# An MLP up projection computed with seven block products instead of eight, with the residual stream kept in DRAM

## The chip, the cores and the metric

The kernel runs on one core of a Trainium2 chip. The metric is the device time of one execution in microseconds (us), lower is better. Its engines are named as the profile names them: PE (TensorE matmuls), PEld (TensorE weight loads), DVE (VectorE), ACT (ScalarE), POOL (GpSimd) and SP (SyncE, which issues nearly all transfers). Each engine works through its own instructions in the order of the program and waits for others by semaphores; a compiler-side scheduler fixes that order when the kernel is built.

## What is computed

One layer of a hybrid backbone for 512 latent tokens (and 256 context tokens) with 2048 channels: two groups of recurrent heads, an output projection, then an MLP with a depthwise convolution on an 8 x 64 grid. All data is 32-bit float. The change is in the MLP:

```python
def conv_ffn(h, rows, cols, w_up, conv_w, conv_b, w_down):
    u = jnp.einsum('btd,df->btf', h, w_up)                 # 2048 -> 2 x 5504
    u_gate, u_val = jnp.split(u, 2, axis=-1)
    g = lax.conv_general_dilated(u_gate.reshape(b, rows, cols, D_FF), conv_w[:, :, None, :], ...)
    g = g.reshape(b, t, D_FF) + conv_b
    return jnp.einsum('btf,fd->btd', jax.nn.silu(g) * u_val, w_down)
...
    x = x + gt1 * merge_groups(lat_gla, lat_ml, lat_gates[0], lat_gates[1], ...)
    h2 = rmsnorm(x, g_norm2) * (1 + sc2) + sh2
    x = x + gt2 * conv_ffn(h2, rows, GRID_W, w_up, conv_w, conv_b, w_down)
    return rmsnorm(x, g_final)
```

`sc2`, `sh2`, `gt1` and `gt2` come from a modulation, a product of one vector with a 2048 x 12288 matrix.

## The kernel before

Channels or features lie on the 128 partitions, tokens along the free dimension. The 2048 channels are 16 tiles of 128 (`KT`), the 5504 MLP features 43 tiles (`NF`), the tokens 512 columns (`T`).

Precision. PE multiplies in a reduced float format. `split` (L88) makes two parts of a tensor: ACT casts it to the high part (line L89 of the profile), DVE subtracts that from the original for the low part (L90). `mm3` (L104) then runs three matmuls for one product: high weight with high data, high weight with low data, low weight with high data. The third is the first that reads the low part of the weight. `mm` (L95) is the line of nearly all matmuls in the profile.

Weights. `load_split` (L160) is the only way in for weights: a transfer of 512 KB on SP into one of four `wraw` buffers, then a split into one of two `whi` and one of two `wlo` buffers. A split can therefore run one load ahead of PE. `unit` (L186) multiplies 16 channel tiles by up to four output tiles and takes eight such loads. After each load it runs a few `fillers`: pieces of the modulation (`mod_chunk`, L242), each with a transfer into `wraw`, a sum on DVE, a scaling on ACT and a sum of 512 columns on POOL (L257). `rate` says how many run per load. Of the modulation's parts, 2, 3 and 4 are made ahead of the MLP and part 5 (`gt2`) during its first units.

Stages. After the heads come the gate projections (`ga` in the profile), the output projection (`wo`) and the residual stream `x2`, 16 tiles in SBUF. Its norm gives `h2`, held as 16 high and 16 low tiles. The MLP then runs over eleven groups of up to four feature tiles (`QUADS`). `up_gate` (L1028) makes the gate features of a group (`ug`): ACT copies each from PSUM into a padded grid `pad`, ACT makes the first of nine convolution taps, DVE the other eight (L1043), ACT the SiLU. `up_val` (L1048) makes the value features (`uv`); DVE multiplies (L83) and the result is split into `gh` and `gl`, the input of the down projection. After two groups of up work `down_block` (L1064) runs for four blocks of 512 output channels (`dn`) and adds the result, times `gt2`, to `x2` (`residual`, L952). The last three groups go down together, and the last block of them (`dl`) is cut in two token ranges, so that the final norm can begin early.

All loads, splits, taps and matmuls are ordered by the scheduler; parts under `tc.high_priority()` come first where they are ready. PSUM has six accumulators of 512 columns for this.

Of the kernel before, what the change touches and what calls it, by code (L numbers as in the profile page):

```python
# [11 lines left out]
F32 = mybir.dt.float32  # L12
F32R = mybir.dt.float32r
# [5 lines left out]
P = 128  # L19
# [17 lines left out]
QUADS = [4] * 10 + [3]  # L37
GROUPS = [[0, 1], [2, 3], [4, 5], [6, 7], [8, 9, 10]]
# [31 lines left out]
def block_kernel(ctx: ExitStack, tc: tile.TileContext, a: dict, out: bass.AP):  # L70
# [48 lines left out]
    actp = pool(ctx, "actp")  # L119
    yp = pool(ctx, "yp")  # L120
    psA = pool(ctx, "psA", 6, PSUM)
# [16 lines left out]
    def ytile(k, name, shape=(P, T)):  # L138
        return yp.tile(list(shape), F32, name=name, tag=f"y{k}")
# [18 lines left out]
    rate, credit = [0], [0]  # L158

# [82 lines left out]
    def mod_chunk(region, n, kp, parts):  # L242

        name = f"m{region}_{n}_{kp}"
        raw = wraw.tile([P, 2, T], F32, name=f"raw_{name}", tag="raw")
        nc.sync.dma_start(raw, a["w_mod2"][region - 2, n, kp])
        if kp == 0:
            parts += [sum_tile(i, name) for i in range(2)]
        dv, po = parts
        ce, co = (csil[:, 2 * kp + i : 2 * kp + i + 1] for i in range(2))  # L250
        if kp == 0:
            V.tensor_scalar(out=dv, in0=raw[:, 0, :], scalar1=ce, scalar2=None, op0=ALU.mult)
            S.activation(po, raw[:, 1, :], AF.Copy, scale=co)
        else:
            V.scalar_tensor_tensor(out=dv, in0=raw[:, 0, :], scalar=ce, in1=dv, op0=ALU.mult, op1=ALU.add)  # L255
            S.activation(raw[:, 1, :], raw[:, 1, :], AF.Copy, scale=co)  # L256
            G.tensor_tensor(out=po, in0=po, in1=raw[:, 1, :], op=ALU.add)  # L257
        if kp == KP - 1:
            G.tensor_tensor(out=po, in0=po, in1=dv, op=ALU.add)
# [616 lines left out]
    mod_fillers((2, 3, 4), 3)  # L876
# [34 lines left out]
    for h in range(1, 2 * H):  # L911
        if h + 1 < 2 * H:
            accs = [acc(f"a{h + 1}_{g}", BANKS[g]) for g in range(6)]
            steps = project_steps(h + 1, accs)
        else:
            rate[0] = 1.5
            accs = [acc(f"ga0_{i}") for i in range(4)]
            steps = unit_steps(a["w_gates"][0], "ga0", *hx, accs)
        weave(first_stages(tiles) if h == 1 else stages(h, tiles), steps)
        for _ in steps:  # L920
            pass
        if h + 1 < 2 * H:
            tiles = evict(h + 1, accs)
# [8 lines left out]
    rate[0] = 1.5  # L932
# [19 lines left out]
    def residual(k, ps, gate, sl=slice(0, T)):  # L952
        xx = x2[k][:, sl]
        V.scalar_tensor_tensor(out=xx, in0=ps, scalar=gate[:, k : k + 1], in1=xx, op0=ALU.mult, op1=ALU.add)
# [27 lines left out]

    sums2 = []
    for n in range(4):
        accs = unit(a["w_out"][n], f"wo{n}", yh, yl)
        with tc.high_priority():
            for i in range(4):
                residual(4 * n + i, accs[i], modc[2])
                square(4 * n + i, sums2, rp, "sq")
# [3 lines left out]
    h2 = ([], [])  # L993
    with tc.high_priority():
        for k in range(KT):
            t = gp.tile([P, T], F32, name=f"h2_{k}", tag="h2")
            sk, bk = modc[4][:, k : k + 1], modc[3][:, k : k + 1]
            h2[0].append(acttile(k, "h", f"h2h{k}"))
            h2[1].append(acttile(k, "l", f"h2l{k}"))
            mul(t, x2[k], r2)  # L1000
            S.activation(h2[0][k], t, AF.Identity, scale=sk, bias=bk)  # L1001
            V.tensor_scalar(out=t, in0=t, scalar1=sk, scalar2=bk, op0=ALU.mult, op1=ALU.add)
            sub(h2[1][k], t, h2[0][k].bitcast(F32))
    st_3.close()
    st_h.close()


    fp = pool(ctx, "fp")
    tp = pool(ctx, "tp", 4)
# [4 lines left out]
    pads = [fp.tile([P, ROWS + 2, GW + 2], F32, name=f"pad{i}") for i in range(4)]  # L1014
    for p in pads:
        G.memset(p, 0.0)
    gs = {}
    LAST = 4 * GROUPS[-1][0]
    glast = fp.tile([P, NF - LAST, P], F32, name="glast")

    def sum_tile(i, name):
        return fp.tile([P, T], F32, name=f"sum{i}_{name}", tag=f"g{'hl'[i]}10")

    rate[0] = 1.5
    fillers += [lambda: None] * 20
    mod_fillers((5,), 2)

    def up_gate(q):  # L1028
        accs = unit(a["w_up4"][2 * q] if q < 10 else a["w_up3"][0], f"ug{q}", *h2, n=QUADS[q])
        convs = []  # L1030
        for i, ps in enumerate(accs):
            f = 4 * q + i
            with tc.high_priority():
                S.copy(pads[i][:, 1 : ROWS + 1, 1 : GW + 1], ps.rearrange("p (r c) -> p r c", c=GW))
            t = tp.tile([P, T], F32, name=f"cv{f}", tag="cv")
            t3 = t.rearrange("p (r c) -> p r c", c=GW)
            for tap in range(9):
                src = pads[i][:, tap // 3 : tap // 3 + ROWS, tap % 3 : tap % 3 + GW]
                w = cwt[:, f, tap : tap + 1]
                if tap == 0:  # L1040
                    S.activation(t3, src, AF.Identity, scale=w, bias=cbt[:, f : f + 1])  # L1041
                else:
                    V.scalar_tensor_tensor(out=t3, in0=src, scalar=w, in1=t3, op0=ALU.mult, op1=ALU.add)  # L1043
            S.activation(t, t, AF.Silu)
            convs.append(t)
        return convs

    def up_val(q, convs):  # L1048
        accs = unit(a["w_up4"][2 * q + 1] if q < 10 else a["w_up3"][1], f"uv{q}", *h2, n=QUADS[q])
        for i, ps in enumerate(accs):  # L1050
            f = 4 * q + i
            with tc.high_priority():
                mul(convs[i], convs[i], ps)
                gh = fp.tile([P, T], F32R, name=f"gh{f}", tag=f"gh{f % 8 if q < 10 else 8 + i}")
                gl = fp.tile([P, T], F32R, name=f"gl{f}", tag=f"gl{f % 8 if q < 10 else 8 + i}")
                split(gh, gl, convs[i])
            gs[f] = (gh, gl)
            if f >= LAST:
                S.copy(glast[:, f - LAST, :], convs[i][:, 3 * P :])

    def fspan(qs):
        return [f for q in qs for f in range(4 * q, 4 * q + QUADS[q])]

    def down_block(fs, blk):  # L1064
        accs = [acc(f"dn{fs[0]}_{blk}_{i}") for i in range(4)]
        for p in range(0, len(fs), 2):
            pair = fs[p : p + 2]
            wh, wl = load_split(a["w_down"][blk][:, pair[0] : pair[0] + len(pair), :], f"d{pair[0]}_{blk}", n=len(pair))
            for i in range(4):
                for ff, f in enumerate(pair):  # L1070
                    mm3(accs[i], wh[:, ff, P * i : P * i + P], wl[:, ff, P * i : P * i + P],
                        gs[f][0], gs[f][1], f == fs[0], f == fs[-1])
        with tc.high_priority():
# [15 lines left out]
    fs = fspan(todo[0])  # L1089
    parts = [slice(0, 3 * P), slice(3 * P, T)]  # L1090
    sums3 = [[], []]
    for blk in range(3):
        down_block(fs, blk)
        for k in range(4 * blk, 4 * blk + 4):
            for pt, sl in enumerate(parts):
                square(k, sums3[pt], fp, f"fq{pt}", sl)
            S.activation(x2[k], x2[k], AF.Copy, scale=gnf[:, k : k + 1])

    wd = []
    for n, f in enumerate(fs):  # L1100
        if n < 10:
            raw = actp.tile([P, T], F32, name=f"raw_dl{f}", tag=f"a{'hl'[n % 2]}{11 + n // 2}")
        else:
            raw = fp.tile([P, T], F32, name=f"raw_dl{f}", tag="wlast")
        wh, wl = acttile(n, "h", f"dlh{f}"), acttile(n, "l", f"dll{f}")
# [5 lines left out]
    for pt, sl in enumerate(parts):  # L1111
# [10 lines left out]
        with tc.high_priority():  # L1122
            for i in range(4):
                residual(12 + i, accs[i], modc[5], sl)
                square(12 + i, sums3[pt], fp, f"fq{pt}", sl)
            r3 = token_rstd(sums3[pt], fp, f"rmsf{pt}", w)
            r3s = fp.tile([P, w], F32, name=f"r3s{pt}", tag=f"r3s{pt}")
# [17 lines left out]
def arrange(x, c, ctx, c_ctx, w_mod, b_mod, g_norm1, g_norm2, w_in, gla_w_lr, gla_b_lr, mlstm_b_gate,  # L1145
# [44 lines left out]
    for d in range(2):  # L1190
# [3 lines left out]
    r["w_up4"] = np.stack([blocks(w_up[:, FF * s + 512 * q : FF * s + 512 * q + 512], 512)  # L1194
                           for q in range(10) for s in range(2)])
    r["w_up3"] = np.stack([blocks(w_up[:, FF * s + 5120 : FF * s + 5504], 384) for s in range(2)])
# [20 lines left out]
```

## Time and profile before

| | us |
|---|---|
| median of 3 runs | 2595.97 (2594.4 to 2598.1) |
| profiled execution | 2598.67 |
| its span | 2597.0 |
| mean granted PE clock | 0.993 of full |

The time is that of the whole execution; the span runs from its first to its last recorded instruction, so 1.7 us lie around it. The page gives the busy time of each engine and the chain of work that ended last. Matmuls are pipelined: the mean length of one matmul record (some 390 ns for 512 columns) is longer than the distance between two of them, and it is the distance that counts. The lines themselves are shown where the prediction uses them.

### The profile page before, as it was taken

How to read it: one execution, taken by the hardware profiler on the slowest of the kernel's cores; microseconds unless marked ns; L12 is line 12 of the kernel's file. 1: busy time of each engine (PE TensorE's matmuls, PEld its weight loads, DVE VectorE, ACT ScalarE, POOL GpSimd, SP SyncE). 2: the span in 40 equal slices, each digit the busy share in tenths (PEclk: the TensorE clock that was granted, in tenths of full speed). 3: DMA queues.
4: the chain of work that ended last, by engine and by line, in shares of the span. 5: the costliest groups of instructions: out<-in, count | busy, mean ns of one | idle time of the engine just before them, and what ended most of it. 6: DMA issues, size and time to landing. Idle time of an engine off the chain costs nothing.

```text
span 2597.0 us, 31782 instructions
## 1 busy us (share of the span) xinstructions
PE 2530.0 (97%) x12782; PEld 2132.0 (82%) x12782; DVE 1361.3 (52%) x1972; ACT 873.7 (34%) x1289; POOL 225.8 (9%) x179
## 2 busy tenths in 40 slices
PE   6998999999999999999999999999999999999998
PEld 4887898888897887878878888888888888888887
DVE  6566765543344465458576326533653365336643
ACT  4224543333334344334443123312331233123431
POOL 0000000111212323210321000000000000000000
PEclk9999999999999999989999999999999999999999
DMA  8751012231333566633554333333233323333431
GB/s 322 282 204 41 30 44 81 69 96 64 130 119 126 205 233 221 192 121 100 208 186 138 97 98 98 98 97 97 98 97 96 96 95 97 97 97 90 141 90 65
DMA packets 96676, 321.96 MB, mean 124 GB/s; under 512 B 11152, under 2 KB 15504, under 8 KB 96528
## 3 DMA queue, kind: packets, MB, share of 16 engines
q1 hardware_dynamic: 95376, 319.40, 37.5%
q8 instruction: 100, 1.64, 0.3%
q10 hardware_dynamic: 1152, 0.52, 0.1%
q14 instruction: 48, 0.39, 0.0%
HBM read 315.69 MB, written 4.19 MB: 123 GB/s over the span
## 4 chain that ended last, share of the span: by engine, by line
PE 89%; DVE 5%; DMA 3%; issue 1%; ACT 1%; SPq 0%; POOL 0%; DVEq 0%; ACTq 0%; POOLq 0%
PE ug L95 18%; PE uv L95 17%; PE dn L95 17%; PE a L95 16%; PE wo L95 6%; PE ga L95 5%; PE po L95 3%; DMA raw_m<-in_w_mod 2%; PE sl L95 1%; PE dl L95 1%; PE ps_m L95 1%; DVE cv L1043 1%; DMA raw_h<-in_w_heads 1%; PE s L95 0%; PE cst L95 0%
## 5 line engine op out<-in xcount | busy, mean ns | idle before, releaser
L95 PE MATMUL ug<-h2h,hi_ug 128*128 128x512 f32 x688 | 269.0, 392 | 1.6 <-ACT h2h L1001 1.6
L95 PE MATMUL uv<-h2h,lo_uv 128*128 128x512 f32 x688 | 268.8, 391 | 1.6 <-DVE lo_uv L90 1.6
L95 PE MATMUL uv<-h2h,hi_uv 128*128 128x512 f32 x688 | 268.6, 390 | 1.2 <-ACT hi_uv L89 1.2
L95 PE MATMUL ug<-h2l,hi_ug 128*128 128x512 f32 x688 | 268.3, 390 | 0.0
L95 PE MATMUL uv<-h2l,hi_uv 128*128 128x512 f32 x688 | 268.2, 390 | 0.0
L95 PE MATMUL ug<-h2h,lo_ug 128*128 128x512 f32 x688 | 268.2, 390 | 0.0
L95 PE MATMUL dn<-gh,hi_d 128*128 128x512 f32 x644 | 250.5, 389 | 0.0
L95 PE MATMUL dn<-gl,hi_d 128*128 128x512 f32 x644 | 250.5, 389 | 0.0
L95 PE MATMUL dn<-gh,lo_d 128*128 128x512 f32 x644 | 250.5, 389 | 0.0
L1043 DVE SCALAR_TENSOR_TENSOR cv<-pad,cwt,cv 128x512 f32<-128x512 f32 x344 | 242.5, 762 | 10.6 <-ACT cv L1041 9.1
L90 DVE TENSOR_TENSOR lo_ug<-raw_ug,hi_ug 128x1024 fp32r<-128x1024 f32 (+1 forms) x88 | 106.5, 1210 | 240.1 <-ACT hi_ug L89 240.1
L257 POOL TENSOR_TENSOR sum_m<-sum_m,raw_m 128x512 f32<-128x512 f32 x112 | 175.3, 1566 | 578.2 <-ACT raw_m L256 358.4
L90 DVE TENSOR_TENSOR lo_uv<-raw_uv,hi_uv 128x1024 fp32r<-128x1024 f32 (+1 forms) x88 | 105.9, 1203 | 177.5 <-ACT hi_uv L89 177.1
L90 DVE TENSOR_TENSOR lo_d<-raw_d,hi_d 128x1024 fp32r<-128x1024 f32 x82 | 98.8, 1205 | 166.5 <-ACT hi_d L89 165.5
L89 ACT CAST hi_ug<-raw_ug 128x1024 fp32r<-128x1024 f32 (+1 forms) x88 | 90.9, 1033 | 266.6 <-PE ug L95 196.4
L89 ACT CAST hi_d<-raw_d 128x1024 fp32r<-128x1024 f32 x82 | 85.0, 1037 | 280.4 <-PE dn L95 231.8
L255 DVE SCALAR_TENSOR_TENSOR sum_m<-raw_m,csil,sum_m 128x512 f32<-128x512 f32 x112 | 97.6, 871 | 156.1 <-DMA raw_m<-in_w_mod 155.9
L89 ACT CAST hi_uv<-raw_uv 128x1024 fp32r<-128x1024 f32 (+1 forms) x88 | 90.9, 1033 | 246.4 <-PE uv L95 181.3
L95 PEld LDWEIGHTS uv<-h2h,lo_uv 128*128 128x128 f32 x688 | 129.4, 188 | 30.2 <-DVE lo_uv L90 3.2
L95 PEld LDWEIGHTS ug<-h2h,hi_ug 128*128 128x128 f32 x688 | 129.8, 189 | 28.8 <-ACT h2h L1001 1.9
L95 PEld LDWEIGHTS uv<-h2h,hi_uv 128*128 128x128 f32 x688 | 129.5, 188 | 28.3 <-ACT hi_uv L89 1.6
L95 PEld LDWEIGHTS ug<-h2h,lo_ug 128*128 128x128 f32 x688 | 129.6, 188 | 27.2
(308 smaller groups left out, 5178.7 us busy)
## 6 DMA issues: line engine op xcount, KB each, us to landing
raw_m<-in_w_mod SPq DMA_DIRECT2D x192, 512.0 KB, 4.4
raw_ug<-in_w_up SPq DMA_DIRECT2D x80, 512.0 KB, 3.4
raw_uv<-in_w_up SPq DMA_DIRECT2D x80, 512.0 KB, 3.4
raw_d<-in_w_down SPq DMA_DIRECT2D x79, 512.0 KB, 3.5
raw_h<-in_w_heads SPq DMA_DIRECT2D x64, 512.0 KB, 3.4
raw_ga<-in_w_gates SPq DMA_DIRECT2D x32, 512.0 KB, 4.3
raw_wo<-in_w_out SPq DMA_DIRECT2D x32, 512.0 KB, 4.3
xl<-in_xT SPq DMA_DIRECT2D x16, 256.0 KB, 5.1
```

Of the source, the lines that this page charges most:

```text
L89: S.copy(hi, x)
L90: return V.tensor_tensor(out=lo, in0=x, in1=hi.bitcast(F32), op=ALU.subtract).ins
L95: ins = PE.matmul(*args, **kw)
L255: V.scalar_tensor_tensor(out=dv, in0=raw[:, 0, :], scalar=ce, in1=dv, op0=ALU.mult, op1=ALU.add)
L257: G.tensor_tensor(out=po, in0=po, in1=raw[:, 1, :], op=ALU.add)
L1043: V.scalar_tensor_tensor(out=t3, in0=src, scalar=w, in1=t3, op0=ALU.mult, op1=ALU.add)
```

## The change

It has five parts.

1. **Seven products for eight.** For feature tiles 2 to 42 the gate and the value of one tile are computed together (`up_seven`). The weight of a tile is seen as four quarters: gate or value (the rows of the block matrix) by lower or upper eight channel tiles, `a11`, `a12` (gate), `a21`, `a22` (value), each 128 x 1024 and 512 KB. The data is four blocks: lower or upper channel tiles by first or second 256 tokens. Strassen's scheme in Winograd's form takes seven block products in place of eight, at the price of sums. Four sums of data blocks (`tsrc`, `bt`) are made once, on POOL, and split. Four sums of weight quarters are made for every feature tile, on POOL (`gt`): `s1 = a21 + a22`, `a21 = a11 - a21`, `a11 = s1 - a11`, `a12 = a12 - a11`. Each product has its own split of 1024 columns and 24 matmuls of 256 columns. ACT copies intermediate results out of PSUM (`p1`, `u2`, `p5`), DVE adds three of them to others on the way to `pad` and `val`.
2. **Tiles 0 and 1** are made as before (`up_first`), 512 columns or two halves of 256 at a time, while the data sums are being made.
3. **Buffers.** The quarters go through six slots, four in `wraw` and two in a freed operand half (`spare`), which also holds `s1`. There are two `pad` and two `cv` buffers instead of four.
4. **The residual stream lies in DRAM** (`x2d`) during the MLP: it is written after the output projection; each down block loads four tiles (`stage`), adds and writes them back; all 16 come back before the last group.
5. **Groups and fillers.** Down projections run after groups of seven feature tiles (the last has eight), after the up work of the next tile. Part 5 of the modulation moves ahead of the MLP, with rates of 2 and 2.25 per load instead of 1.5, into transfer buffers of their own (`mraw3`).

```diff
-QUADS = [4] * 10 + [3]
-GROUPS = [[0, 1], [2, 3], [4, 5], [6, 7], [8, 9, 10]]
+FIRST = 2
+GROUPS = [list(range(7 * n, 7 * n + 7 + (n == 5))) for n in range(6)]
...
-    mod_fillers((2, 3, 4), 3)
+    mod_fillers((2, 3, 4, 5), 3)
...
-    rate[0] = 1.5
+    modraw[0] = pool(st_3, "mraw3", 4)
+    rate[0] = 2.25
...
+                nc.sync.dma_start(x2d[k], x2[k])
...
+    for k in range(KH):
+        u, v = x2[k], x2[KH + k]
+        gt(u[:, lo], u[:, hi], u[:, lo])
+        gt(u[:, hi], v[:, hi], u[:, hi])
+        gt(v[:, hi], v[:, hi], u[:, lo])
+        gt(v[:, lo], v[:, lo], v[:, hi])
...
+    def quarter(f, j):
+
+        n = slot[0] % 6
+        slot[0] += 1
+        if n % 3 == 2:
+            q = spare[0][:, n // 3, :]
+        else:
+            q = wraw.tile([P, KH * P], F32, name=f"q{f}_{j}", tag="raw")
+        nc.sync.dma_start(q, a["w_up"][f - FIRST, j // 2, j % 2].rearrange("p k c -> p (k c)"))
+        return q
+
+    def up_seven(f):
+
+        a11, a12, a21, a22 = (quarter(f, j) for j in range(4))
+        s1 = spare[1][:, 0, :]
+        gt(s1, a21, a22, ALU.add)
+        gt(a21, a11, a21)
+
+        def product(n, src, o, first):
+            wh = whi.tile([P, KH * P], F32R, name=f"hi_q{f}_{n}", tag="hi")
+            wl = wlo.tile([P, KH * P], F32R, name=f"lo_q{f}_{n}", tag="lo")
             with tc.high_priority():
+                split(wh, wl, src)
+            for k in range(KH):
+                c = slice(P * k, P * k + P)
+                mm3(o, wh[:, c], wl[:, c], *operands[n](k), first and k == 0, k == KH - 1, skip_group_check=True)
...
+        product(0, a11, x, True)
+        with tc.high_priority():
+            S.copy(p1, x)
+        product(1, a12, w, True)
+        gt(a11, s1, a11)
+        with tc.high_priority():
+            add(pad[:, 1 : ROWS // 2 + 1, 1 : GW + 1], rows(w), rows(p1))
+        gt(a12, a12, a11)
+        product(2, a11, x, False)
+        with tc.high_priority():
+            S.copy(u2, x)
+        product(3, s1, v, True)
+        with tc.high_priority():
+            S.copy(p5, v)
+        product(4, a21, x, False)
+        with tc.high_priority():
+            add(val[:, hi], x, p5)
+        product(5, a12, v, False)
+        with tc.high_priority():
+            add(pad[:, ROWS // 2 + 1 : ROWS + 1, 1 : GW + 1], rows(v), rows(u2))
+        product(6, a22, x, False)
+        with tc.high_priority():
+            S.copy(val[:, lo], x)
+        conv(f, pad, val)
...
+    def down_block(fs, blk):
+        for i in range(4):
+            nc.sync.dma_start(stage[i], x2d[4 * blk + i])
+        accs = down_products(fs, blk)
         with tc.high_priority():
             for i in range(4):
-                residual(4 * blk + i, accs[i], modc[5])
+                residual(stage[i], 4 * blk + i, accs[i], modc[5])
+                nc.sync.dma_start(x2d[4 * blk + i], stage[i])
...
-    for q in range(len(QUADS)):
-        convs = up_gate(q)
-        if len(todo) > 1 and q > todo[0][-1]:
-            assert not fillers
+    for f in range(FIRST, NF):
+        up_seven(f)
+        if len(todo) > 1 and f > todo[0][-1]:
             for blk in range(4):
-                down_block(fspan(todo[0]), blk)
+                down_block(todo[0], blk)
             todo.pop(0)
-        up_val(q, convs)
```

`conv` in the changed kernel is the tap loop of `up_gate` for one tile, followed by the product with `val` and the split.

More of the change, by code (lines that the diff above doesn't have):

```diff
@@ L992, in block_kernel @@
     assert not fillers
[L993 to L1003, printed above, removed]
     st_3.close()
     st_h.close()
+    st_a.close()
+    KH, TH = KT // 2, T // 2
     fp = pool(ctx, "fp")
-    tp = pool(ctx, "tp", 4)
+    tp = pool(ctx, "tp", 2)
     cwt = fp.tile([P, NF, 9], F32, name="cwt")
```

185 lines of the change are left out of this document (120 added, 65 removed).

## Prediction

> **What bounds the kernel now.** First the page: the span, the busy time of PE (TensorE), and the shares of the chain that ended last.
>
> ```profile
> span 2597.0 us, 31782 instructions
> PE 2530.0 (97%) x12782; PEld 2132.0 (82%) x12782; DVE 1361.3 (52%) x1972; ACT 873.7 (34%) x1289; POOL 225.8 (9%) x179
> PE 89%; DVE 5%; DMA 3%; issue 1%; ACT 1%; SPq 0%; POOL 0%; DVEq 0%; ACTq 0%; POOLq 0%
> ```
>
> PE carries 89% of the chain; POOL is nearly unused, DVE half used. Then the chain in order of time, for the MLP (start, length, work):
>
> ```profile
> 1163.54 46.03 PE ug L95 x192
> 1209.58 43.52 PE uv L95 x192
> ...
> 1393.25 87.04 PE dn L95 x384
> 1480.29 43.52 PE uv L95 x192
> ...
> 2459.49 89.76 PE dn L95 x396
> 2549.25 13.37 PE dl L95 x77
> ```
>
> A matmul that streams 512 columns costs 43.52/192 = 0.22667 us. One feature tile (gate and value) has 96 of them, 21.76 us; one tile of the down projection has 48, 10.88 us. The MLP up to 2549.25 takes 1385.7 us. Its pure matmul time is 43 x 21.76 + 1932 x 0.22667 = 1373.6 us, so 12.1 us are lost, all of it early. The windows show where (length, busy time of PE, PEld, DVE, ACT, POOL, granted clock, DMA share, GB/s):
>
> ```profile
> 1163.54:1209.58 46.04, 46.04 (x193) 37.93 (x194) 37.20 (x57) 22.38 (x28) 2.42 (x4) 0.95 0.30 91
> 1209.58:1393.25 183.67, 180.90 (x801) 148.46 (x801) 124.48 (x149) 76.68 (x98) 52.94 (x32) 0.99 0.54 183
> 1480.29:1654.37 174.08, 174.08 (x769) 144.14 (x769) 73.67 (x85) 49.85 (x58) 0.00 (x0) 1.00 0.32 97
> ```
>
> The first is 2.5 us over 43.52, the second 9.6 us over 4 x 43.52, while the modulation fillers run; afterwards PE is full, with DVE busy 42% and POOL at zero. So PE has nothing left to gain but fewer columns, and DVE and POOL have room, if they can use it together.
>
> **The change: columns and loads on PE.** Per tile, seven products of 8 x 3 matmuls, 256 columns wide: 168 instead of 96. That width is in the trace already, in the head projections:
>
> ```profile
> 553.31 0.28 PE L95 MATMUL a<-hi_h,hTl 128*128 128x256 f32 x1
> 553.32 0.19 PEld L95 LDWEIGHTS a<-hi_h,hTh 128*128 128x128 f32 x1
> 553.43 0.28 PE L95 MATMUL a<-hi_h,hTh 128*128 128x256 f32 x1
> ...
> 553.55 0.28 PE L95 MATMUL a<-lo_h,hTh 128*128 128x256 f32 x1
> ```
>
> Starts are 0.12 us apart, with a new weight load for each. A product is 24 x 0.12 = 2.88 us, a tile 20.16 us: 1.60 us less than 21.76, or 66 us over 41 tiles. That is all PE can give. [...]
>
> **What DVE and POOL get.** Per tile there were four weight splits of 1024 columns; now there are seven, and the eight convolution taps, the product with the value and the split of the result stay. Three sums out of PSUM are added. POOL, idle until now, gets four sums of 1024 columns. The durations (mean ns of one) and pitches (starts of neighbours in the timeline):
>
> ```profile
> L90 DVE TENSOR_TENSOR lo_ug<-raw_ug,hi_ug 128x1024 fp32r<-128x1024 f32 x80 | 98.8, 1236 | 218.6 <-ACT hi_ug L89 218.6
> L89 ACT CAST hi_ug<-raw_ug 128x1024 fp32r<-128x1024 f32 x80 | 84.2, 1052 | 243.9 <-PE ug L95 180.3 <-PE uv L95 32.9 <-issue 26.2
> ...
> 1308.38 4.05 DVE L1043 SCALAR_TENSOR_TENSOR cv<-pad,cwt,cv 128x512 f32<-128x512 f32 x6
> ...
> 1347.72 0.68 DVE L90 TENSOR_TENSOR gl<-cv,gh 128x512 fp32r<-128x512 f32 x1
> 1348.32 0.68 DVE L83 TENSOR_TENSOR cv<-cv,uv 128x512 f32<-128x512 f32 x1
> ...
> 1349.52 1.22 DVE L90 TENSOR_TENSOR lo_ug<-raw_ug,hi_ug 128x1024 fp32r<-128x1024 f32 x1
> 1350.65 0.69 DVE L90 TENSOR_TENSOR gl<-cv,gh 128x512 fp32r<-128x512 f32 x1
> ...
> L1138 POOL TENSOR_TENSOR x<-x,r3s 128x384 f32<-128x384 f32 x4 | 3.9, 1012 | 1199.5 <-ACT r3s L1128 1199.5
> L1138 POOL TENSOR_TENSOR x<-x,r3s 128x128 f32<-128x128 f32 x4 | 1.7, 456 | 7.1 <-ACT r3s L1128 7.1
> ```
>
> A split costs DVE 1.13 us, a tap 4.05/6 = 0.675, the two operations of 512 columns 0.60 each: 7 x 1.13 + 8 x 0.675 + 1.2 = 14.5 us per tile. POOL takes (1012 - 456)/256 = 2.17 ns per column, so 456 + 896 x 2.17 = 2.40 us for 1024 columns, an estimate from these two rows; 9.6 us per tile. Each alone fits into 20.16 us. Together they don't, for this reason (timeline of POOL, then of DVE, at the same places):
>
> ```profile
> 1057.38 1.30 POOL L257 TENSOR_TENSOR sum_m<-sum_m,raw_m 128x512 f32<-128x512 f32 x1 [2.33 <-ACT raw_m L256]
> ...
> 1232.95 2.16 POOL L257 TENSOR_TENSOR sum_m<-sum_m,raw_m 128x512 f32<-128x512 f32 x1 [31.04 <-ACT raw_m L256]
> ...
> 1311.44 3.94 POOL L257 TENSOR_TENSOR sum_m<-sum_m,raw_m 128x512 f32<-128x512 f32 x1 [12.42 <-ACT sum_m L253]
> ...
> 1232.73 1.23 DVE L90 TENSOR_TENSOR lo_uv<-raw_uv,hi_uv 128x1024 fp32r<-128x1024 f32 x1
> 1233.87 2.58 DVE L1043 SCALAR_TENSOR_TENSOR cv<-pad,cwt,cv 128x512 f32<-128x512 f32 x2
> ...
> 1313.02 1.21 DVE L90 TENSOR_TENSOR lo_uv<-raw_uv,hi_uv 128x1024 fp32r<-128x1024 f32 x1
> 1314.16 3.10 DVE L1043 SCALAR_TENSOR_TENSOR cv<-pad,cwt,cv 128x512 f32<-128x512 f32 x3
> ```
>
> A POOL sum of 512 columns takes 1.30 us alone. The one at 1232.95 begins under a DVE split, ends 1.30 us after that split, and the two taps behind it take 2.58 us instead of 2 x 0.675 + 0.08 = 1.43: 1.15 us later, what is left of the POOL sum. At 1311.44 POOL waits 2.65 us through DVE's work and then delays the three taps by 1.0 us. So a POOL sum and a DVE operation that reads two SBUF tensors take turns, whole instruction by whole instruction. All 14.5 us of DVE above are of that kind. **A tile then needs 14.5 + 9.6 = 24.1 us of taking turns, more than 20.16 on PE and more than 21.76 before.** Six of 7 tiles between down stages are such tiles.
>
> **The order that decides the rest.** POOL's rows for tile 11 and the first of tile 12 (q11_0, q11_1, q11_3 are the quarters a11, a12, a22, spareh here a21, sparel the sum s1); before, POOL has no row between the last modulation sum and the last stage:
>
> ```order
> L1042 TENSOR_TENSOR sparel_10125<-spareh_10124,q11_3_12732 128x1024
> L1042 TENSOR_TENSOR spareh_10124<-q11_0_12727,spareh_10124 128x1024
> L1042 TENSOR_TENSOR q11_0_12727<-sparel_10125,q11_0_12727 128x1024
> L1042 TENSOR_TENSOR q11_1_12729<-q11_1_12729,q11_0_12727 128x1024
> L1042 TENSOR_TENSOR sparel_10125<-q12_2_12964,q12_3_12966 128x1024
> ```
>
> Three sums in a row stand ahead of product 2. DVE in before, at the start of a gate unit (lo_ug5 are its weight splits):
>
> ```order
> L90 TENSOR_TENSOR lo_ug5_1_13468<-raw_ug5_1_13466,hi_ug5_1_13467 128x1024
> L90 TENSOR_TENSOR gl19_13429<-cv19_12645,gh19_13428 128x512
> L90 TENSOR_TENSOR lo_ug5_2_13498<-raw_ug5_2_13496,hi_ug5_2_13497 128x1024
> L90 TENSOR_TENSOR lo_ug5_3_13528<-raw_ug5_3_13526,hi_ug5_3_13527 128x1024
> L90 TENSOR_TENSOR lo_ug5_4_13558<-raw_ug5_4_13556,hi_ug5_4_13557 128x1024
> ```
>
> and in the changed kernel, at the start of tile 12 (lo_q12_n is the split for product n, cv11 the taps of the tile before):
>
> ```order
> L90 TENSOR_TENSOR lo_q12_0_12975<-q12_0_12961,hi_q12_0_12974 128x1024
> L1073 SCALAR_TENSOR_TENSOR cv11_12945<-pad1_9547,cwt_9542,cv11_12945 128x512 x3
> L90 TENSOR_TENSOR lo_q12_1_13004<-spareh_10124,hi_q12_1_13003 128x1024
> L1073 SCALAR_TENSOR_TENSOR cv11_12945<-pad1_9547,cwt_9542,cv11_12945 128x512 x2
> L90 TENSOR_TENSOR lo_q12_2_13035<-q12_0_12961,hi_q12_2_13034 128x1024
> L1073 SCALAR_TENSOR_TENSOR cv11_12945<-pad1_9547,cwt_9542,cv11_12945 128x512
> L86 TENSOR_TENSOR pad0_9546<-w12_12971,part_p1_9679 128x4x64
> L1073 SCALAR_TENSOR_TENSOR cv11_12945<-pad1_9547,cwt_9542,cv11_12945 128x512
> L90 TENSOR_TENSOR lo_q12_3_13064<-sparel_10125,hi_q12_3_13063 128x1024
> ```
>
> Splits that stood alone now have taps between them, and a split that waits for POOL holds up the taps behind it.
>
> **The cycle of one tile.** Six raw slots serve four quarters, so the last quarter a22 of the next tile takes the place of this tile's a12, which is free after split 5; the transfer is the one of this row (KB, us to landing):
>
> ```profile
> raw_ug<-in_w_up SPq DMA_DIRECT2D x80, 512.0 KB, 3.4
> ```
>
> Count from the end of product 3. The cast and split for product 5 end at 1.05 + 1.2 = 2.3; a22 lands at 5.7; s1 is done at 8.1. From there s1's two followers on POOL (4.8) and, taking turns with them, split 0 (1.13), three taps (2.03), split 1 (1.13) and two taps (1.35) fill 10.4 us in any order: 18.5. The cast for product 2 ends at 19.6; POOL's fourth sum holds until 20.9, split 2 ends at 22.1. Product 2 still needs 2.88 - 0.24 us after it (its third matmul is the first to read the split): 24.7. Product 3 ends at 27.6, and the cycle closes. If split 2 gets ahead of the fourth sum it is 26.4, if the taps behind then wait, 28.4. I take **27.6 us**, with 24.1 (the turns alone) and 29 as ends.
>
> **The sum,** against the profiled execution, 2598.67 us with a span of 2597.0. The first tile after each of the five down stages finds its sums made ahead and no taps left: PE's 20.16 and a little for hand-overs, 20.5. Tile 2 must wait for the space of an operand half that up_first reads, then a transfer, three sums, and the leftover splits and taps of tiles 0 and 1 on DVE: s1 can't start before 3.4 us, and 18 half splits (0.34 each, half of the 0.68 above), two splits, seven taps and three sums, 20 us of turns, stand ahead of split 2. Products 2 to 6 (14.4 us) follow: about 36 (30 to 45). up_first, where half the depth is streamed at 256 columns (192 x 0.12 + 96 x 0.22667 = 44.8 us instead of 43.52), also gets 24 POOL sums of 256 columns (0.73 us each by the slope above) and 14 half splits on a DVE already busy 37.2 of 46 us: 52 (47 to 60). The other 35 tiles take 966 us. Down blocks: 1968 matmuls, 446.1 us; the stage's loads and stores of the stream have a block of 84 x 0.22667 = 19 us each, and the next block's weights are queued ahead of them, so I cost them at nothing (without that cover 3.4 us a block, 68 us in all). Together 52 + 36 + 966 + 102.5 + 446.1 = 1602.6, against 1385.7: +216.9. The last block has 8 tiles instead of 11:
>
> ```profile
> L95 PE MATMUL dl<-glast,raw_dl 128*128 128x128 f32 x88 | 10.9, 278 | 0.0
> ```
>
> 36 matmuls less of 13.37/77 = 0.174 us and 24 less of 10.9/88 = 0.124: -9.2. The fillers moved forward add 0.75 of a chunk per weight load in the gate and output projections; their extra buffers let the weights go on, so +3 (-3 to +15). 2598.67 + 216.9 - 9.2 + 3 = 2809; the median of the runs shown, 2595.97, lies 2.7 lower, so **2807**.
>
> **Rivals.**
> - *The turns alone set the pace,* 24.1 to 26 us a tile: DVE and POOL would have to fill each other's gaps, also those behind the 3.4 us transfer. 2687 at the low end. Chance 0.22.
> - *PE cools in the stalls.* About 7.5 us of each 27.6 are idle. The window with the longest gap in PE's work shows a lower clock:
>
> ```profile
> 1130.00:1163.00 33.00, 29.26 (x136) 24.74 (x134) 12.34 (x20) 8.03 (x12) 0.00 (x0) 0.87 0.24 80
> ```
>
> At 0.87, products 2 and 3 in the cycle take 0.9 us longer, the others a little: about 29.1 us, 2860. Chance 0.18. [...]
> - *Faster: PE sets the pace after all.* It takes POOL and DVE running at once in the up stage; then the cycle above has no turns: the cast for product 2 (1.05), products 2 and 3 (5.76), split 5 (2.3), the transfer (3.4) and three sums (7.2), 19.7 us, with hand-overs (an estimate) up to 21, against PE's 20.16. It decides from 21.8 us a tile downwards. 46 + 41 x 20.16 + 446.1 against 1385.7 gives 2525, with 21 us a tile 2560. The timelines above speak against it. Chance 0.06.
> - [...] Chance 0.01; then the change doesn't do what it says, since fewer columns would not be less work on PE.
>
> The forecast itself, 2750 to 2845, gets 0.50, the remaining 0.03 is a worse start-up. The range runs from the turns alone (2687) and a shorter start to the cooled clock with the upper ends of start-up and fillers: 2670 to 2895. Faster by over 0.2% 0.06, within 0.2% (about what a measurement of this kernel can tell) 0.02, slower 0.92.
>
> **What would show it.** Up matmuls at 0.12 us starts; DVE splits of 1024 columns and POOL sums well over 1.23 and 2.4 us in the record, since they include the wait for each other; PE's idle time ended mostly by splits lo_q (DVE) and casts hi_q that wait for POOL, at products 1 and 2; tiles 27 to 28 us apart, those after a down stage near 20.5; no idle time in the down blocks. Tiles at 20 us with DVE and POOL busy at once would make the prediction wrong; at 24 us only its cycle.

## The result

| | before | after |
|---|---|---|
| median | 2595.18 us (4 runs, 2590.07 to 2598.1) | 2815.43 us (4 runs, 2812.44 to 2823.45) |
| profiled execution, span | 2598.67, 2597.0 us | 2812.44, 2810.7 us |
| mean granted PE clock | 0.993 | 0.957 |

The changed kernel takes 1.0856 times as long, 95% interval 1.0827 to 1.0885. The page of the changed kernel: its span, the busy times, and the shares of the chain that ended last.

```profile
span 2810.7 us, 39386 instructions
PE 2547.4 (91%) x15806; PEld 2283.1 (81%) x15806; DVE 1882.1 (67%) x2277; ACT 1028.5 (37%) x1569; POOL 717.6 (26%) x381
PE 48%; DVE 16%; issue 4%; ACT 2%; DMA 2%; POOL 1%; DVEq 0%; SPq 0%; POOLq 0%; ACTq 0%
```

PE's busy time is almost what it was, but the span is 214 us longer: PE waits. For whom is told by the table of PE's waits (total us, times, longest):

```profile
PE w L95 <- DVE lo_q L90: 151.7, 41, 5.9
PE x L95 <- DVE lo_q L90: 26.9, 45, 1.6
```

`w` is the accumulator of product 1 alone; products 0, 2, 4 and 6 share `x`. So once in each of the 41 tiles PE waits for split 1, 3.7 us on the mean, and hardly anywhere else. The costliest groups show what DVE and POOL do meanwhile (total us, mean ns of one, then the idle time ahead):

```profile
L1073 DVE SCALAR_TENSOR_TENSOR cv<-pad,cwt,cv 128x512 f32<-128x512 f32 x344 | 463.7, 1349 | 5.1
L90 DVE TENSOR_TENSOR lo_q<-q,hi_q 128x1024 fp32r<-128x1024 f32 x165 | 241.9, 1466 | 77.9 <-ACT hi_q L89 77.8
L1042 POOL TENSOR_TENSOR q<-q,q 128x1024 f32<-128x1024 f32 x28 | 80.9, 2888 | 36.2 <-issue 26.1 <-DVE lo_q L90 9.1
```

These are means: a tap that takes 0.75 us alone is recorded at 1.35 (single taps at 0.73 to 2.92), a split of 1.22 at 1.47, a sum of 2.41 (the mean of the thirteen that are like the first row of the timelines below) at 2.89. The chain in order of time, for the MLP:

```profile
1178.78 7.98 PE u L95 x43
...
1407.18 76.20 PE dn L95 x336
...
1594.19 4.39 PE w L95 x22
1598.59 3.06 PE x L95 x24
...
1621.29 4.38 PE w L95 x22
1665.64 75.98 PE dn L95 x335
...
2444.53 76.20 PE dn L95 x336
...
2703.96 65.31 PE dn L95 x288
2769.27 10.31 PE dl L95 x59
```

The distance of the two `w` rows is one tile, 27.10 us. Between the starts of two down stages lie (2444.53 - 1407.18)/4 = 259.3 us; less the stage's own 76.2 that is 183.1 us for seven tiles, **26.2 us on average**. Of these seven the first behind a down stage takes 21.4 to 22.8 us, the others 26.9 on the mean (from the first matmul of one tile to that of the next). The average of 26.2, worked out in the same way from each kernel's own down stages, is the yardstick of the experiments below. One tile in the timelines, POOL's rows first, then DVE's (start, length, and in brackets the idle time ahead of the row and what ended it):

```profile
1610.22 2.42 POOL L1042 TENSOR_TENSOR sparel<-q,spareh 128x1024 f32<-128x1024 f32 x1 [13.17 <-DMA spareh<-in_w_up]
1612.71 3.29 POOL L1042 TENSOR_TENSOR q<-spareh,q 128x1024 f32<-128x1024 f32 x1
1616.08 2.68 POOL L1042 TENSOR_TENSOR spareh<-sparel,spareh 128x1024 f32<-128x1024 f32 x1
1621.36 2.77 POOL L1042 TENSOR_TENSOR q<-q,spareh 128x1024 f32<-128x1024 f32 x1 [2.60 <-issue]
...
1592.92 1.22 DVE L90 TENSOR_TENSOR lo_q<-spareh,hi_q 128x1024 fp32r<-128x1024 f32 x1
...
1605.55 1.23 DVE L90 TENSOR_TENSOR lo_q<-spareh,hi_q 128x1024 fp32r<-128x1024 f32 x1 [1.08 <-ACT hi_q L89]
...
1611.13 2.60 DVE L90 TENSOR_TENSOR lo_q<-spareh,hi_q 128x1024 fp32r<-128x1024 f32 x1 [0.54 <-ACT hi_q L89]
1613.65 6.45 DVE L1073 SCALAR_TENSOR_TENSOR cv<-pad,cwt,cv 128x512 f32<-128x512 f32 x3
1620.01 1.22 DVE L90 TENSOR_TENSOR lo_q<-q,hi_q 128x1024 fp32r<-128x1024 f32 x1
1621.15 3.53 DVE L1073 SCALAR_TENSOR_TENSOR cv<-pad,cwt,cv 128x512 f32<-128x512 f32 x2
```

POOL is idle for 13 us, until a22 lands at 1610.2. Then three sums follow each other, s1 at 1610.22 and its two followers. DVE's split 0 (1611.13) meets the first, and takes 2.60 instead of 1.22; the three taps behind it meet the other two, and take 6.45 instead of the 2.1 that three of 0.75 us need when they start 0.675 us apart. Split 1, the one at 1620.01, has its input from 1613.96 on, where ACT's cast for it ends (a row of ACT's timeline: start 1612.91, length 1.05), but stands behind those taps. It ends at 1621.23, and PE's product 1 goes on at 1621.29.

The cycle can be read off these rows: the split 1 of one tile earlier ends at 1594.14, product 1 takes 4.4 us, product 2 3.06, product 3 2.83 (24 x 0.118), then the cast and split for product 5 end at 1606.78; then come 3.4 us to a22's landing, 2.4 us for s1, and 8.6 us to the end of the next split 1.

Two windows show the clock (length, busy time of PE, PEld, DVE, ACT, POOL, granted clock, DMA share, GB/s):

```profile
1591.00:1594.10 3.10, 0.00 (x0) 0.00 (x0) 3.06 (x4) 1.32 (x2) 0.67 (x1) 1.00 0.00 0
1594.19:1597.59 3.40, 3.40 (x16) 3.40 (x17) 3.37 (x3) 0.00 (x0) 2.77 (x1) 0.51 0.00 0
1597.60:1601.00 3.40, 3.40 (x28) 3.23 (x28) 3.40 (x5) 1.05 (x1) 0.00 (x0) 0.99 0.36 95
```

PE stands still before product 1, for 4.45 us in this tile; the granted clock is then half (0.51) for 3.4 us, in which 16 matmuls start, and full again (0.99) for the next 28. In other tiles the half clock lasts longer: behind the stall that ends at 1305.69 matmuls start 0.21 us apart for 5.3 us, at a granted clock of 0.50, before they return to 0.12. Product 1 mostly takes 4.4 to 5.1 us in the chain instead of 22 x 0.12 = 2.64.

### The profile page after: what moved, and what is told of

Read it like the earlier page. It is cut to its first block, busy times and chain, and to the rows that moved or that the text cites. A ratio compares the mean times of both kernels' runs of the same rounds, so it can differ in the third digit from the quotient of the medians.

```text
span 2810.7 us, 39386 instructions
## 1 busy us (share of the span) xinstructions
PE 2547.4 (91%) x15806; PEld 2283.1 (81%) x15806; DVE 1882.1 (67%) x2277; ACT 1028.5 (37%) x1569; POOL 717.6 (26%) x381
## 4 chain that ended last, share of the span: by engine, by line
PE 48%; DVE 16%; issue 4%; ACT 2%; DMA 2%; POOL 1%; DVEq 0%; SPq 0%; POOLq 0%; ACTq 0%
PE dn L95 16%; PE x L95 9%; PE v L95 8%; DVE cv L1073 7%; DVE lo_q L90 6%; PE wo L95 6%; PE w L95 5%; PE ga L95 2%; DMA raw_m<-in_w_mod 2%; ACT hi_q L89 1%; PE dl L95 1%; POOL x L1042 1%; DVE sum_m L257 0%; PE po L95 0%; POOL sum_m L259 0%
## 5 line engine op out<-in xcount | busy, mean ns | idle before, releaser
L1073 DVE SCALAR_TENSOR_TENSOR cv<-pad,cwt,cv 128x512 f32<-128x512 f32 x344 | 463.7, 1349 | 5.1
L90 DVE TENSOR_TENSOR lo_q<-q,hi_q 128x1024 fp32r<-128x1024 f32 x165 | 241.9, 1466 | 77.9 <-ACT hi_q L89 77.8
L89 ACT CAST hi_q<-q 128x1024 fp32r<-128x1024 f32 x165 | 173.1, 1049 | 307.1 <-POOL q L1042 86.3
L95 PE MATMUL w<-b1h,lo_q 128*128 128x256 f32 x328 | 127.8, 390 | 151.7 <-DVE lo_q L90 151.7
L90 DVE TENSOR_TENSOR lo_q<-spareh,hi_q 128x1024 fp32r<-128x1024 f32 x81 | 128.7, 1589 | 41.6 <-ACT hi_q L89 41.6
L95 PE MATMUL a<-hi_h,hTh 128*128 128x256 f32 x512 | 150.3, 294 | 0.0
L95 PE MATMUL a<-lo_h,hTh 128*128 128x256 f32 x512 | 145.0, 283 | 0.0
L95 PE MATMUL a<-hi_h,hTl 128*128 128x256 f32 x512 | 144.9, 283 | 0.0
L95 PEld LDWEIGHTS dn<-gh,lo_d 128*128 128x128 f32 x656 | 123.1, 188 | 25.6
L95 PEld LDWEIGHTS dn<-gh,hi_d 128*128 128x128 f32 x656 | 123.1, 188 | 25.4
```

The lines of the kernel that those rows point to most:

```text
L89: S.copy(hi, x)
L90: return V.tensor_tensor(out=lo, in0=x, in1=hi.bitcast(F32), op=ALU.subtract).ins
L95: ins = PE.matmul(*args, **kw)
```

## The experiments

Each kernel starts from the changed kernel where nothing else is said. First, whether the sums' dependencies or their mere presence cost the time. **The sums made, but read by nobody** (the products take the quarters as loaded, so the up projection is not computed):

```diff
-        gt(a21, a11, a21)
+        gt(s1, a11, a21)
...
-        gt(a11, s1, a11)
+        gt(s1, a22, a11)
...
-        gt(a12, a12, a11)
+        gt(s1, a12, a22)
...
-        product(3, s1, v, True)
+        product(3, a22, v, True)
```

> POOL makes its four sums per tile at the same place, after the same transfer, but into a tile that no product reads; the products take the quarters as loaded (so the up projection's values are not computed). The chain sums -> split 2 is gone, the turns between POOL and DVE remain. Theory of turns: a regular tile takes 24.1 to 25.5 us (14.5 of DVE + 9.6 of POOL), time 2705 to 2760. Rival, the chain of transfer and three sums alone, with POOL and DVE at once: PE sets the pace at 20.2 to 20.6 us a tile, time near 2575. [...]

Measured 2878.61 us, ratio 1.108 (1.1048 to 1.1112), 27.9 us a tile: slower still, which no theory had said. The timelines of POOL and DVE in this kernel tell why:

```profile
1655.95 2.64 POOL L1042 TENSOR_TENSOR sparel<-spareh,q 128x1024 f32<-128x1024 f32 x1 [14.41 <-DMA q<-in_w_up]
1658.67 3.26 POOL L1042 TENSOR_TENSOR sparel<-q,spareh 128x1024 f32<-128x1024 f32 x1
1662.01 6.03 POOL L1042 TENSOR_TENSOR sparel<-q,q 128x1024 f32<-128x1024 f32 x2
...
1662.94 6.44 DVE L1073 SCALAR_TENSOR_TENSOR cv<-pad,cwt,cv 128x512 f32<-128x512 f32 x3
1669.29 1.22 DVE L90 TENSOR_TENSOR lo_q<-q,hi_q 128x1024 fp32r<-128x1024 f32 x1
```

With nothing to hold them, all four sums run in one row as soon as a22 is there, and all four now stand ahead of split 1, the fourth too, which in the changed kernel overwrites the input of split 1 and so comes after it (1621.36): from the landing to split 1's end it takes 14.6 us (1655.95 to 1670.51) instead of 11.0. So it is not a sum's result that product 1 waits for. It waits for a split that stands behind taps, which wait for POOL.

**The four sums left out** (here too the products take the quarters as loaded):

```diff
-        gt(s1, a21, a22, ALU.add)
-        gt(a21, a11, a21)
...
-        gt(a11, s1, a11)
...
-        gt(a12, a12, a11)
...
-        product(3, s1, v, True)
+        product(3, a22, v, True)
```

> The four sums per tile are left out; the products take the quarters as loaded (so the up projection's values are not computed). Theory of turns and theory of the chain: neither is left, PE sets the pace at 20.2 to 20.8 us a tile, time 2550 to 2600, PE at full clock in the up stage. If the narrow matmuls or their 168 weight loads were the cause, the tile would stay at 27 us and the time near 2815.

Measured 2539.8 us, ratio 0.9776 (0.9748 to 0.9805), a little below the expected range, 19.74 us a tile: 168 matmuls at 0.1175 us, with hardly a wait in between. The chain has these starts of the first and the fifth down stage:

```profile
1363.13 76.19 PE dn L95 x336
...
2220.71 76.19 PE dn L95 x336
```

The four sums therefore cost 2815 - 2540 = 275 us, of which 6.4 us for each of the 41 tiles are the yardstick's share.

**24 more matmuls between products 0 and 1,** to keep PE busy there; their result isn't used:

```diff
+        dummy = psb(f"warm{f}", (P, TH))
+        for k in range(3 * KH):
+            mm(dummy, b1[0][:, k % KH, 0:P], b1[0][:, k % KH, lo], start=k == 0, stop=k == 3 * KH - 1)
```

> The changed kernel with 24 additional matmuls of 256 columns between products 0 and 1 (2.88 us, into a free PSUM bank, on data that is ready), where PE waits 4 to 6 us for split 1 and then runs product 1 at half clock. Theory of turns: split 2 sets the pace, whatever product 1 costs; the tile stays at 26.5 to 27.5 us, time 2795 to 2830, although product 1 is back at 0.12 us a matmul. Rival, PE's clock sets the pace: product 1 gets 1.8 to 2.4 us shorter, 35 tiles, time 2730 to 2755.

Measured 2911.27 us, ratio 1.1206 (1.1173 to 1.1239), mean clock 0.979, 28.6 us a tile. Both theories missed. The scheduler also gave DVE another order, all eight taps and the multiply ahead of split 3, and the waits moved with it. PE also has 2.8 us more to do in each tile. So the run doesn't separate the clock from the order. It shows only that the tile does not become short with the clock near full (0.97 over the seven tiles from 1497.8 on, against 0.93 over the seven from 1483.3 on in the changed kernel).

Then what the sums meet. **The sums on VectorE:**

```diff
+        def gv(o, x, y, op=ALU.subtract):
+            V.tensor_tensor(out=o, in0=x, in1=y, op=op)
...
-        gt(s1, a21, a22, ALU.add)
-        gt(a21, a11, a21)
+        gv(s1, a21, a22, ALU.add)
+        gv(a21, a11, a21)
```

(and the other two in the same way)

> The four sums per tile move from POOL to DVE, where one of 1024 columns costs 1.13 us instead of 2.4, and nothing is left that takes turns. DVE then has 14.5 + 4.5 + 1.2 = 20.2 us per tile, all behind one another. Theory of turns: a regular tile takes 20.5 to 22.5 us, time 2570 to 2650. If the amount of work on DVE and POOL together were the cause, not the turns, DVE with more to do than before would keep the tile at 27 us or above, 2815 or more.

Measured 2630.08 us, ratio 1.0134 (1.0114 to 1.0155), 21.6 us a tile, inside the range. A sum takes DVE 1.13 us where it takes POOL 2.4, and with POOL idle nothing is held any more: the taps are back at 750 ns on the mean, the splits at 1220.

**The taps accumulate in PSUM,** so that a tap reads one tensor from SBUF, not two:

```diff
-        t = tp.tile([P, T], F32, name=f"cv{f}", tag="cv")
+        t = psb(f"cv{f}")
...
-        mul(t, t, val)
+        o = tp.tile([P, T], F32, name=f"ov{f}", tag="cv")
+        mul(o, t, val)
...
-        split(*gs[f], t)
+        split(*gs[f], o)
```

> The convolution taps accumulate in a PSUM bank instead of SBUF, so that a tap and the product with the value read one SBUF tensor and don't take turns with POOL; sums stay on POOL. Theory of turns: taps take 0.7 us again whatever POOL does, what remains in turns is 8.5 + 9.6 us, and the splits 0 and 1 still wait for sums; a tile takes 22 to 24.5 us, time 2640 to 2725. If only the number and place of the POOL sums mattered (their latency), the tile would stay near 27 us, time near 2815.

Measured 2722.16 us, ratio 1.0489 (1.0468 to 1.051), 24.0 us a tile, inside the range. Two groups of this kernel, the splits and the taps:

```profile
L90 DVE TENSOR_TENSOR lo_q<-q,hi_q 128x1024 fp32r<-128x1024 f32 x165 | 273.3, 1657 | 121.4 <-ACT hi_q L89 121.2
L1073 DVE SCALAR_TENSOR_TENSOR cv<-pad,cwt,cv 128x512 f32<-128x512 f32 x344 | 256.9, 749 | 5.0
```

The taps fall from 1349 to 749 ns with the same sums on POOL beside them, where the kernel without sums has 751: they no longer meet. The splits, which still read two SBUF tensors, now bear more of it (1657 ns against 1466). The half-tile adds of the changed kernel, with one input in PSUM and the result in SBUF, take 409 to 429 ns, beside a sum or not. So an operation that reads two SBUF tensors is held here, and one that reads one of its two inputs from PSUM isn't; that the hold lasts to the end of the sum is seen in split 0 of the timelines above, whose 2.60 us are the 1.51 to the end of the first sum and 1.09 of its own.

Then when the sums can start. **The quarters loaded in another order,** so that the next a22 takes the slot that split 4 leaves:

```diff
-        a11, a12, a21, a22 = (quarter(f, j) for j in range(4))
+        a11, a21, a12, a22 = (quarter(f, j) for j in (0, 2, 1, 3))
```

> The changed kernel with one thing altered: the four quarters of a tile are loaded in the order a11, a21, a12, a22 instead of a11, a12, a21, a22, so that the last quarter of the next tile takes the buffer that split 4 leaves and not the one that split 5 leaves, some 2.9 us earlier. Work, sums and their order are the same. Theory 'place' (the sums fall together on the three taps that stand ahead of split 1, because they all wait for the last quarter; it is where they fall that costs, not how many): with the first sum 2.9 us earlier, part of the bunch falls beside other work, the regular tile goes from 27.1 to 24.1 to 25.5 us, the run from 2815 to 2690 to 2760 us, and product 1's wait for split 1 shrinks from 3.7 us to under 2. Rival 'turns' (the sum of what GpSimd and VectorE do in turn sets the tile wherever it falls): tile still 26.5 to 27.5 us, 2790 to 2820 us. Rival 'clock' (the tile is locked to the two-state TensorE clock): the tile stays at 27.3 us.

Measured 2768.62 us, ratio 1.0666 (1.0645 to 1.0688), 25.1 us a tile on average: the right side, but 9 us short of the range, and with 2.3 us of waiting for split 1 in each tile (96.0 us over 41), not under 2. The same edit with the taps in PSUM:

> The changed kernel with the taps in PSUM and the quarters loaded as a11, a21, a12, a22; the sums stay on GpSimd in their order. It closes a table of two by two: late or early last quarter, taps in SBUF or PSUM (2815 and 2769 us with the taps in SBUF, 2722 us with the taps in PSUM and the late quarter). If the early quarter works by letting the sums fall beside work that they don't meet, and the taps in PSUM take the largest part of that meeting away already, it brings less here than the 46 us there: 2690 to 2715 us. If instead the transfer's landing is by itself what the sums wait for, it brings as much or more: 2640 to 2685 us.

Measured 2668.85 us, ratio 1.0278 (1.0253 to 1.0303), 22.7 us a tile: as much as there, the second of the two cases. And with the sums on VectorE:

> The changed kernel with the four sums on VectorE and the quarters loaded as a11, a21, a12, a22. The sums on VectorE alone gave 2630 us (tile 21.4 us), with VectorE held in its line by the first sum's wait for the last quarter (3.8 us at the longest). Theory 'the wait in VectorE's line is what is left': the last quarter lands 2.9 us earlier, the wait goes, the tile is 20 to 20.8 us and the run 2565 to 2605 us. Rival 'VectorE is full' (8 taps at 0.75, 7 splits at 1.22, 4 sums, 3 half-tile adds and the multiply are some 22 us): no change, 2620 to 2640 us.

Measured 2591.02 us (10 runs, 2588.05 to 2595.63), ratio 0.9983 (0.9974 to 0.9993), 20.7 us a tile, inside the range, but not in the way expected: DVE's waits for the transfer at s1 add up to 17.0 us, against 19.1 with a22 late. What fell are its waits for ACT's casts, from 59.4 to 27.8 us in all; why they fell is open. It is the only kernel with the sums that is not slower than before: 4.7 us below it, which is within 0.2%. The three edits stand in a table (us; us a tile):

| | a22 late | a22 early | difference |
|---|---|---|---|
| sums on POOL, taps in SBUF | 2815.4; 26.2 | 2768.6; 25.1 | 46.8 |
| sums on POOL, taps in PSUM | 2722.2; 24.0 | 2668.9; 22.7 | 53.3 |
| sums on DVE, taps in SBUF | 2630.1; 21.6 | 2591.0; 20.7 | 39.1 |

The early quarter brings about the same in each row, even where POOL has no sums at all. So my reason for it, that the bunch of sums then falls beside other work, isn't borne out. The transfer can begin one product (2.8 us) earlier, and 0.9 to 1.3 us a tile are gained; by which wait, these runs don't show. The taps in PSUM bring 93 and 100 us, also in both columns.

**Two steps further with the sums on POOL.** With the taps in PSUM, a21 can be made as a22 minus the new a11, after that one, so that fewer sums stand ahead of split 1:

```diff
-        gt(a21, a11, a21)
...
+        gt(a21, a22, a11)
```

First with s1 moved to VectorE, and a22 late:

> As the run with the taps in PSUM, and the first sum s1 on DVE, and a21 made as a22 minus the new a11, after a11, so that POOL's first sum is the one product 2 waits for. Theory of turns: 8.5 + 1.1 + 7.2 us in turns, DVE 16.7 us in all; PE sets the pace nearly, 20 to 21.5 us a tile, time 2545 to 2620, perhaps faster than the kernel before. A rival cause outside the tiles (start of the up stage, modulation fillers) would keep it above 2650.

Measured 2624.93 us, ratio 1.0114 (1.0088 to 1.014), 5 us above the range, 21.7 us a tile. DVE's waits in this kernel show s1 in its line, waiting for the transfer, with all that is queued behind it:

```profile
DVE sparel L1129 <- DMA q<-in_w_up: 29.3, 23, 3.7
```

Then with all sums on POOL and a22 early:

> The changed kernel with three things altered: the taps accumulate in a bank of PSUM (so a tap reads one SBUF tensor, not two), the quarters are loaded as a11, a21, a12, a22, and a21 is replaced by a22 minus the new a11 after that one is made, so that two sums, not three, wait to be made between the last quarter's landing and split 1. What it computes is unchanged. Theory 'place and port': GpSimd's sums keep only splits and the half-tile adds from their turn; the tile is 20 to 21.7 us against 24.3 with the taps in PSUM alone, and the run 2540 to 2625 us. Rival 'turns': splits 8.6, adds 1.3 and sums 9.6 in turn are 19.5 us and the taps 6.0 beside them, so nothing is left to wait for except order: 2540 to 2580. Rival 'the transfer is late anyway': as with the taps in PSUM alone, 2690 to 2725 us.

Measured 2611.21 us, ratio 1.0057 (1.004 to 1.0074), 21.3 us a tile, inside the first range. That is 58 us under the kernel with taps in PSUM and the early a22, with the same four sums on POOL, from one sum's place in the order (and its inputs).

**One sum back on POOL,** from the fastest kernel: taps in PSUM, the last sum on POOL, the other three on VectorE.

```diff
-        gv(a12, a12, a11)
+        gt(a12, a12, a11)
```

> The kernel with the four sums on VectorE and the early last quarter (2591 us; VectorE works back to back there, 20.55 us a tile, so VectorE is its bound), with two things altered: the taps accumulate in PSUM, and the fourth sum, a12 minus the new a11, goes back to GpSimd. Theory 'place' (a GpSimd sum costs VectorE only what it meets there that reads two SBUF tensors): VectorE's own work falls by 1.15 us to 19.4 us, and the sum of 2.4 us falls partly beside taps, so the tile is 19.8 to 20.3 us, limited by TensorE's own 19.74, and the run 2560 to 2585 us. Rival 'turns' (the whole 2.4 us are taken from VectorE wherever it falls): 19.4 plus 2.4 is 21.8 us, 2625 to 2650 us. Rival 'nothing': 2586 to 2600 us.

Measured 2626.4 us, ratio 1.0111 (1.0095 to 1.0128), 21.5 us a tile: the rival "turns" named it. In the timelines of this kernel the sum meets just the split of product 2:

```profile
1551.95 2.41 POOL L1042 TENSOR_TENSOR q<-q,q 128x1024 f32<-128x1024 f32 x1 [18.74 <-DVE lo_q L90]
...
1552.85 2.59 DVE L90 TENSOR_TENSOR lo_q<-q,hi_q 128x1024 fp32r<-128x1024 f32 x1 [0.37 <-ACT hi_q L89]
```

DVE gives 1.13 us of work away and gets back 1.37 us of waiting in that split (2.59 against 1.22), with another 0.37 us ahead of it, where it waits for ACT's cast. At this place POOL doesn't pay even for one sum; beside taps it wasn't tried. The run differs from the fastest kernel in two things: the taps take 750 ns in both, so their move to PSUM shows no cost on DVE, but the move without the sum was not run, and that all of the 35 us come from the sum is not shown.

Last, a part that has nothing to do with the tiles. **The kernel before, with only part 5 of the modulation moved ahead of the MLP:**

```diff
-    mod_fillers((2, 3, 4), 3)
+    mod_fillers((2, 3, 4, 5), 3)
...
-    rate[0] = 1.5
+    modraw[0] = pool(st_3, "mraw3", 4)
+    rate[0] = 2.25
...
-    mod_fillers((5,), 2)
```

> The kernel before with one part of the change alone: part 5 of the modulation made ahead of the MLP, at rates 2 and 2.25 with transfer buffers of its own. By the profiles the stage up to the MLP gets 12 to 16 us longer (1178 instead of 1163) and the up stage about 9.6 us shorter: 2594 to 2606, ratio 0.999 to 1.004. If the fillers cost nothing ahead of the MLP, as the sum of the prediction had it within a few us, 2586 to 2592.

Measured 2604.1 us, ratio 1.0037 (1.0026 to 1.0048): 9.6 us over the 2594.47 us of before in the same comparison. In its chain the MLP begins 12.3 us later than before (1163.54). The part is paid in the fastest kernel above too; with it put back it would stand at about 2591 - 10 = 2581 us if it cost the MLP no more there than in the kernel before. That is worked out and wasn't run, and DVE has hardly a gap left there to take it (20.36 of 20.55 us busy in a tile, below). The chain:

```profile
1175.87 46.24 PE ug L95 x192
1222.11 43.52 PE uv L95 x192
```

## Why the prediction was right, step by step

The total, 2807 us, lies 8 us below the measured median. Its terms, against the profiled execution:

| term | predicted us | measured us |
|---|---|---|
| ahead of the MLP | +3 | +15.2 (1178.78 - 1163.54) |
| start of the MLP to the first down stage | 52 + 36 + 5 x 27.6 = 226 | 228.4 |
| the other 35 tiles | 30 x 27.6 + 5 x 20.5 = 930.5 | 915.8 |
| down stages | 446.1 | 446.3 |
| end | -9.2 | -6.3 |

The 915.8 is 2703.96 - 1407.18 less five stages of 76.2. Two errors of 12 to 15 us cancel here, by luck. Two more of 10 to 11 hide in the second row: tiles 0 and 1 take 63.3 us (PE turns to tile 2 at 1242.11), above the 47 to 60 that I allowed, with PE busy for 53.0 of the 62.2 us to 1241.00 at a granted clock of 0.84; tile 2 then takes 26.4 instead of 36. In the third row the tiles behind a down stage take 21.4 to 22.8 us, not 20.5, and the other thirty 26.9 on the mean, not 27.6.

- **PE gains 1.60 us a tile; weight loads hide.** Right, a little more: 19.74 us a tile without sums, against 21.76 before, at 0.1175 us a matmul with a weight load each. The chance of 0.01 stood for weight loads that add to the matmuls' time. No run shows that: a load is mostly recorded at 188 ns in the changed kernel, and in one tile of the fastest kernel (window below) PEld is busy for 20.09 and PE for 20.44 of 20.55 us, at the same time.
- **POOL and DVE take turns.** Right, and shown from both sides: taps that read PSUM stop waiting (749 ns for 1349), and a single sum on POOL costs the split beside it 1.37 us. (In the rows of the kernel before, the sum at 1232.95 ends 1.15 us after the split and not 1.30: 1235.11 less 1233.96; the delay read from them, 1.15, stands.) The 14.5 us of DVE work per tile are right too, but for the three half-tile adds that I had left out: with the four sums there (4 x 1.13) and the adds (3 x 0.34, from start to start) that makes 20.0, and the fastest kernel, DVE back to back, has this window of one tile:

```profile
1537.68:1558.23 20.55, 20.44 (x169) 20.09 (x169) 20.36 (x25) 10.40 (x15) 0.00 (x0) 1.00 0.29 103
```

- **The cycle of 27.6 us.** Right in length (27.10 in the tile shown, 26.9 on the mean) and in its first half: split 5, 3.4 us of transfer, s1, then sums and taps in turn up to split 1, 17.1 us predicted up to there and 1604.5 to 1621.2, 16.7, measured (1604.5 is the end of product 3, from the sum of the products above). The step that failed is the second half. I let PE wait at **split 2**, behind two more taps, the cast and the fourth sum, with 2.6 and 2.9 us of products after them. In the trace PE waits at **split 1**, and product 1 covers what comes behind it. That alone would be 2.64 + 2 x 2.83 = 8.3 us after split 1 instead of my 10.5. Of the waits that I named as signs, those at product 2 are all but missing (26.9 us in all for the four products in `x`).
- **The clock.** As a rival I let it fall to a mean of 0.87, for 1.5 us a tile. It falls to one half (0.51 and 0.50 in the two tiles above), for 3.4 us or more, in product 1, which costs 1.75 to 2.4 us in the chain and lies inside the cycle. This fills the gap left by the step above: forecast and rival were both half right, and that their errors cancel, so that the length comes out, is luck. What the tile would take at full clock with the same order stays open, since the run with more matmuls changed the order.
- **The fillers, +3.** Mis-sized: 15.2 us in the trace, of which 12.3 are the moved part of the modulation by itself (the run of the kernel before with it). Their own buffers don't hide them; I had the upper end of the range at +15.
- **Faster, PE sets the pace.** It needed DVE and POOL at once, and here they take turns (taps at 1349 ns for 750, splits at 1466 for 1220). Its price for that, 2525 to 2560, is met only by the kernel without the sums (2540); with the sums on VectorE the best is 2591.

The turns alone, 24.1 us a tile, from which the range's lower end was made, are reached with the sums on POOL only once the taps are in PSUM (24.0), that is, with part of the turns taken away.

## What to carry to other kernels

An idle engine is room only if its work doesn't have to take turns with the busy one's: here 9.6 us of work on an idle POOL cost 6.4 us a tile, and the same work on the already busier DVE under 2. Look at what stands behind a stalled instruction in its engine's line: the split that PE waited for was ready, and was held by taps that nobody needed yet. Where POOL and VectorE would take turns, let VectorE read one of its inputs from PSUM (for the taps that brought 93 and 100 us here), and keep the sums off the place where the line leads to PE.

## What the runs showed of the hardware

- VectorE operations with one SBUF and one PSUM input weren't held by POOL sums: a tap took 749 ns on the mean beside POOL sums, where the same tap with both inputs in SBUF took 1349 on the mean and 2919 at most, and the half-tile adds took 409 to 429 ns, beside a sum or not.
- When nothing depended on the sums the kernel became slower (2879 against 2815 us): freed of its waits, POOL made its fourth sum ahead of split 1 instead of behind it.
- A stall of some 4.4 us once in a tile was followed by half the PE clock (0.51 and 0.50 granted), for 3.4 us in one tile and 5.3 in another, so that the wait cost more than its own length: product 1 mostly took 4.4 to 5.1 us instead of 2.64.
